# Two transformer blocks on one core: state-space branch with rows by token, its tables ordered behind half of the embeddings, and the input projection done by halves

## The chip, the cores and the metric

The kernel runs on one core of one Trainium2 chip, as one program. The metric is the device time of one execution in microseconds (us). The core's engines are TensorE (PE), VectorE (DVE), ScalarE (ACT), GpSimd (POOL) and SyncE (SP, which issues the DMAs). Each works through its own instructions in order and waits on semaphores for the others.

## The reference

Two blocks run one behind the other on x, 1024 tokens of 1024 channels, in fp32. The change lies in the first one.

```python
def first_block(x, ...):
    x = layer_norm(x, ln_emb_g, ln_emb_b)
    z = x @ w_in                                  # 1024 -> 1984 columns
    xs, gs, cq, ckv, kr, gm = split(z)            # 512, 512, 256, 128, 64, 512
    ys = s5_branch(xs, ...) * silu(gs)
    ym = mla_branch(cq, ckv, kr, cos, sin, ...) * silu(gm)
    u = alpha * x + concat(ys, ym) @ w_out
    return layer_norm(u + sigmoid(u @ w_pg) * (p @ w_pp), ln_g, ln_b)

def s5_branch(u, ...):        # 32 groups of 16 channels, 64 complex states for each group
    # a = exp(dt * A);  x_t = k * (B u_t);  h_t = a * h_(t-1) + x_t
    # y_t = Re(C h_t) + d * u_t;  y = gelu(y);  return y * sigmoid(y @ w_glu + b_glu)
```

The second block (adaptive normalisation, dilated attention, 2-D neighbourhood attention, a convolutional feed-forward network) is the longer part of the program.

## The kernel before

Matmul operands are split into a high and a low part (`split_sb`: a cast, and a subtraction for the rest), and each product is three matmuls (`mm3`, lines 135 to 137: high by high, high by low, low by high). `dense` walks over groups of column tiles `mt` of 128 columns, and for each over the two halves `th` of 512 tokens; a tile of `w_in` takes 8 steps of three matmuls, so 24.

The start of the program normalises x (`xt`, `mv`, `rs`), transposes it on PE (`tp`), scales it on ACT (`y`), casts it on DVE (`xh`) and takes the rest on POOL for odd channel tiles, on DVE for even ones (`xl`). PE also multiplies p by w_pp here (operands `ph` and `pl`, evacuated to `ppo`). DVE does at the same time, in `ssm_tables`, the tables of the state-space branch: `edt*` and `emg*` are exponentials, `ang`, `scs` and `scc` the sines and cosines, `pw` and `pv` the powers, `RA` and `RB` the two factors of the rotation of the scan.

The branch runs in eight units of four groups (`ssm_unit(u)`). Eight tokens times 16 channels are folded onto the 128 partitions, and 128 such steps are left. A unit loads `U`; builds `ES` and `CS` (a product on POOL, one on DVE into `tm`, and their sum on DVE); transposes `ES` on PE (`sps`, line 653, copied by ACT to `EM`); multiplies `CS` with `KR` on PE (`kps`, line 658). From `kps`, `TM` is built on DVE: it holds the influence of eight tokens on each other, so it is `kps` shifted by 0 to 7 places in eight bands of 16 rows, one masked instruction for each shift. Then PE gives `px` (line 690), DVE rotates it with `R` (`xr`), scans (`gg`, with the decay `RH`), rotates back (`h`), and PE adds `TM` by `U` and `CS` by `h` into `py` (lines 711 and 712). ACT applies gelu, and the result is stored.

The order of instructions on every engine is set at build time by a scheduler that walks the program with a timeline of its own. PE puts the remaining tiles of `w_in` (4 to 14), the rest of the attention's inputs and the units between each other. `after(a, b)` keeps b behind a in that order without a wait.

Of the kernel before, what the change touches and what calls it, by code (L numbers as in the profile page):

```python
# [37 lines left out]
CST = {}  # L38
_o = 0
for _n, _w in (("inv_freq", 1), ("sgn", 1), ("shift", 8), ("chan", 16)):  # L40
    CST[_n] = (_o, _w)
    _o += _w
# [5 lines left out]
def ap_of(t, offset, dims):  # L48
    return bass.AP(tensor=t.tensor, offset=t.offset + offset, ap=dims)


class Kernel:
# [112 lines left out]
    def dense(self, groups, src, nk, X, evac, psum, tag="mm", halves=(0, 1), pre=None, after=None, late=0,  # L165
              behind=None):


        n = 0
        for grp in groups:  # L170
            ws = pre or {mt: self.load_w(src(mt), nk * 128) for mt in grp}
            pre = None
            tiles = [(mt, th) for th in halves for mt in grp]

            cuts = [0, late, nk] if late else [0, nk]
            pss = {}
# [99 lines left out]
    def block1(self):  # L276
# [10 lines left out]
        xts, pre = [], {}  # L287
# [10 lines left out]
        for th in range(2):  # L298
# [325 lines left out]
    def ssm_unit(self, u):  # L624
# [1405 lines left out]
def _constants():  # L2030
# [47 lines left out]
def _layout(v):  # L2078
    A = np.ascontiguousarray
    f = {k: np.asarray(x) for k, x in v.items()}  # L2080
    r = {}
# [72 lines left out]
```

## Time and profile before

| what | value |
|---|---|
| median of 3 runs | 2269.06 us (2267.28 to 2270.81) |
| the profiled execution's own time | 2265.56 us |
| its span in the trace | 2263.5 us |
| mean granted TensorE clock | 0.972 |
| PE busy | 2122.7 us (94%) |
| DVE busy | 1502.9 us (66%) |
| POOL busy | 1124.1 us (50%) |
| ACT busy | 969.7 us (43%) |

The busy shares are means over stages with different limits. The branch that changes lies in the first 325 us, where PE has its longest pauses. The profiled execution was 3.5 us quicker than the median.

### The profile page before, as it was taken

The page shows a single profiled execution, that of the slowest core. Times are in us where ns is not written, and L with a number is a line of the kernel's source. Part 1 is how long each engine was busy: PE and PEld are TensorE (multiplying, and loading weights), DVE is VectorE, ACT ScalarE, POOL GpSimd, SP SyncE. Part 2 cuts the span into 40 slices and gives each one's busy share as a digit, 9 for nine tenths or more (in the row PEclk, how much of TensorE's full clock was granted, in tenths as well). Part 3 has the DMA queues.
Part 4 walks back from the last instruction along what each step waited for, and adds up shares of the span by engine and source line. Part 5 has one row for each costly group of instructions (what it writes and reads, how often), then busy time and mean ns, then how long its engine had stood idle before and what let it go on. Part 6 is the DMA issues. An engine that isn't in the chain of part 4 may idle for free.

```text
span 2263.5 us, 29117 instructions
## 1 busy us (share of the span) xinstructions
PE 2122.7 (94%) x10216; PEld 1766.0 (78%) x10216; DVE 1502.9 (66%) x2511; ACT 969.7 (43%) x1717; POOL 1124.1 (50%) x728
## 2 busy tenths in 40 slices
PE   5998999899999989999999898999899999989998
PEld 4776777777877778888887786888688888877887
DVE  8969976652486345545656862435987777777676
ACT  4222345432245356666444442223544444455223
POOL 4625556665554545654423333523455555535471
PEclk8999999999999999999999899999999999999999
DMA  7433345555654555555345545442122222234332
GB/s 274 137 101 108 92 122 177 177 172 182 199 172 166 175 167 170 171 171 150 121 136 158 166 159 181 169 139 102 47 84 84 84 84 84 84 130 135 98 126 80
DMA packets 186973, 313.25 MB, mean 138 GB/s; under 512 B 43512, under 2 KB 85068, under 8 KB 186828
## 3 DMA queue, kind: packets, MB, share of 16 engines
q1 hardware_dynamic: 186828, 311.40, 43.0%
q8 instruction: 80, 1.31, 0.2%
q14 instruction: 65, 0.53, 0.1%
HBM read 225.65 MB, written 80.96 MB: 135 GB/s over the span
## 4 chain that ended last, share of the span: by engine, by line
PE 41%; DVE 6%; DMA 2%; issue 1%; ACT 1%; POOL 1%; SPq 0%; POOLq 0%; DVEq 0%; ACTq 0%
PE u L1704 17%; PE ps L137 4%; PE ps L135 4%; PE ps L136 4%; PE pd L1885 3%; PE pd L136 2%; PE pd L135 2%; PE pd L137 2%; PE po L1386 1%; DMA ox<-o_d 1%; DVE P L90 1%; PE tp L1378 1%; DVE x L86 1%; DMA as<-a_d 1%; DVE a L86 1%
## 5 line engine op out<-in xcount | busy, mean ns | idle before, releaser
L111 POOL TENSOR_TENSOR wl<-wst,wh 128x1024 fp32r<-128x1024 f32 (+2 forms) x159 | 398.3, 2507 | 488.8 <-ACT wh L102 454.4
L102 ACT ACTIVATE wh<-wst 128x1024 fp32r<-128x1024 f32 (+1 forms) x164 | 168.3, 1028 | 274.2 <-PE ps L136 115.2
L83 POOL TENSOR_TENSOR acc<-acc,wa 128x512 f32<-128x512 f32 x84 | 110.5, 1316 | 16.6 <-ACT wa L102 13.3
L135 PE MATMUL ps<-xh,wh 128*128 128x512 f32 x256 | 103.3, 404 | 4.2 <-DVE kb L83 2.7
L135 PE MATMUL ps<-h1h,wh 128*128 128x512 f32 x256 | 102.5, 400 | 2.8 <-DVE qz L86 2.1
L135 PE MATMUL ps<-h0h,wh 128*128 128x512 f32 x256 | 103.9, 406 | 0.6 <-ACT wh L102 0.6
L137 PE MATMUL ps<-h0h,wl 128*128 128x512 f32 x256 | 102.9, 402 | 0.7 <-POOL wl L111 0.6
L136 PE MATMUL ps<-h0l,wh 128*128 128x512 f32 x256 | 103.1, 403 | 0.0
L136 PE MATMUL ps<-h1l,wh 128*128 128x512 f32 x256 | 102.7, 401 | 0.0
L137 PE MATMUL ps<-xh,wl 128*128 128x512 f32 x256 | 102.0, 399 | 0.0
L136 PE MATMUL ps<-xl,wh 128*128 128x512 f32 x256 | 101.9, 398 | 0.0
L137 PE MATMUL ps<-h1h,wl 128*128 128x512 f32 x256 | 101.9, 398 | 0.0
L83 POOL TENSOR_TENSOR tb<-rt,grid 128x384 f32<-128x384 f32 x48 | 43.1, 906 | 117.0 <-DVE mx L886 88.9
L135 PE MATMUL pd<-Ah,wh 128*128 128x512 f32 (+1 forms) x256 | 93.8, 366 | 5.4 <-ACT s L102 5.4
L136 PE MATMUL pd<-Al,wh 128*128 128x512 f32 (+1 forms) x256 | 93.8, 366 | 0.5 <-DVE Al L111 0.5
L137 PE MATMUL pd<-Ah,wl 128*128 128x512 f32 (+1 forms) x256 | 92.8, 366 | 0.0
L83 DVE TENSOR_TENSOR z<-r,wst 128x512 f32<-128x512 f32 x40 | 71.6, 1790 | 24.5 <-POOL wl L111 24.0
L886 DVE CUSTOM_DVE_ANT_0 sp<-sp,tab 128x256 f32<-128x256 f32 (+1 forms) x128 | 52.7, 425 | 41.8 <-PE sp L163 26.4
L90 POOL TENSOR_SCALAR wa<-wa,sc 128x512 f32<-128x512 f32 x36 | 56.9, 1582 | 47.0 <-DMA wa<-in_w_ada 45.3
L111 POOL TENSOR_TENSOR wl<-z,wh 128x1024 fp32r<-128x1024 f32 (+1 forms) x28 | 63.9, 2282 | 30.8 <-ACT wh L102 27.2
L102 ACT ACTIVATE a<-a 128x1024 f32<-128x1024 f32 x22 | 23.4, 1063 | 108.9 <-DVE a L86 108.8
L83 DVE TENSOR_TENSOR s<-s,pd 128x512 f32<-128x512 f32 x76 | 51.0, 681 | 27.9 <-PE pd L137 14.1
(595 smaller groups left out, 7086.3 us busy)
## 6 DMA issues: line engine op xcount, KB each, us to landing
wa<-in_w_ada SPq DMA_DIRECT2D x96, 256.0 KB, 3.1
wst<-in_w_in SPq DMA_DIRECT2D x47, 512.0 KB, 4.0
wst<-in_w_up SPq DMA_DIRECT2D x24, 512.0 KB, 3.3
a_d<-a SPq DMA_DIRECT2D x22, 512.0 KB, 2.6
wst<-in_w_down SPq DMA_DIRECT2D x22, 512.0 KB, 3.6
as<-a_d SPq DMA_DIRECT2D x22, 512.0 KB, 3.6
r<-in_w_up SPq DMA_DIRECT2D x20, 512.0 KB, 3.2
wst<-in_w_out SPq DMA_DIRECT2D x16, 512.0 KB, 3.3
```

The costliest lines, as they stand in the source:

```text
L83: (eng or self.nc.vector).tensor_tensor(out, a, b, op)
L86: self.nc.vector.scalar_tensor_tensor(out, a, s, b, op0=op0, op1=op1)
L90: (eng or self.nc.vector).tensor_scalar(out, a, s1, None, op0=op0)
L102: self.nc.scalar.activation(out, a, f, **kw)
L111: self.last_lo = e.tensor_tensor(lo, y, hi.bitcast(F32), ALU.subtract)
L135: first = mm(ps, wh, xh, start=start, stop=False)
L136: mm(ps, wh, xl, start=False, stop=False)
L137: mm(ps, wl, xh, start=False, stop=stop)
L886: self.nc.vector.tensor_tensor_reduce(out=s, in0=s, in1=tab, scale=-1.0, scalar=-NEG, op0=ALU.add, op1=ALU.min, accum_out=m)
L1378: nc.tensor.transpose(tp[:, g], P[:, g], self.ident)
L1704: nc.tensor.matmul(ps, x[:, s], y[:, k], start=first and n == 0, stop=k == 3 and n == 2, skip_group_check=True)
L1885: nc.tensor.matmul(ps, w[u][:, 128 * k:128 * k + 128], x[v], start=start and k == i == 0, stop=k == 1 and i == 2, skip_group_check=True)
```

## The change

1. Tiles 0 to 3 of `w_in` are one group, so their first half is done for all four before the second half of any.
2. The cast of odd channel tiles of the embeddings is done by ACT, 8 of 16.
3. The nine loads of the tables' inputs are ordered behind the store of the last tile of the first half of the embeddings.
4. `dd`, the skip term, is computed once for all 32 groups.
5. A row of the branch's tiles is token by channel instead of channel by token. `U` is loaded in four DMAs, `ES` and `KR` are laid out with channels innermost, so that `ES` is written without a stride.
6. `TM`: one masked product and one masked sum on DVE write `Z` (shift 0 or 1 by the row's parity), and four copies on ACT, of 32 rows each, put it at its place, shifted by 0, 2, 4, 6. The zeros are written once, by two memsets on POOL.
7. `RH`, a broadcast of the decay over 512 columns, goes from POOL to ACT; the memset of its first column stays.
8. `tm`, `x2`, `xr`, `gg`, `g2` and `h` have two buffers instead of one.

```diff
@@ dense
-            ws = pre or {mt: self.load_w(src(mt), nk * 128) for mt in grp}
+            ws = {mt: pre[mt] if pre and mt in pre else self.load_w(src(mt), nk * 128) for mt in grp}
@@ embeddings, loop over th (half) and ct (tile of 128 channels)
-                self.split_sb(y, XH[th][:, ct, :], XL[th][:, ct, :], "v", "g" if ct % 2 else "v")
-                nc.sync.dma_start(self.xn_d[ct][:, th * 512:(th + 1) * 512], y)
+                self.split_sb(y, XH[th][:, ct, :], XL[th][:, ct, :], "a" if ct % 2 else "v", "g" if ct % 2 else "v")
+                st = nc.sync.dma_start(self.xn_d[ct][:, th * 512:(th + 1) * 512], y)
+            if th == 0:
+                half = st
-        self.ssm_tables()
+        self.ssm_tables(half)
@@ projection
-        self.dense([[0, 1], [2, 3]], src, 8, X, evac, pp, pre=pre)
+        self.dense([[0, 1, 2, 3]], src, 8, X, evac, pp, pre=pre)
@@ ssm_open
+        self.TM = [self.sp2.tile([128, 4, 16, 8], F32, name=f"TM{i}") for i in range(2)]
+        for x in self.TM:
+            self.nc.gpsimd.memset(x, 0.0)
@@ ssm_tables(behind): each of the nine loads alike
-        nc.sync.dma_start(prm, I["ssm_prm"])
+        self.after(behind, nc.sync.dma_start(prm, I["ssm_prm"]))
...
+        self.dd = K("dd", [128, 32, 16])
+        self.tt(self.dd, dsk[:, :, None].to_broadcast([128, 32, 16]),
+                self.cst[:, None, o:o + 16].to_broadcast([128, 32, 16]), ALU.mult)
@@ ssm_unit
-        nc.sync.dma_start(U, ap_of(self.u_d[b], 64 * q * 1024, [[128, 128], [16 * 1024, 4], [1, 128]]))
-
-        ES = T("ES", [128, 4, 16, 8])
+        for g in range(4):
+            nc.sync.dma_start(U[:, g], ap_of(self.u_d[b], (64 * q + 16 * g) * 1024, [[128, 8], [1024, 16], [1, 128]]))
+
+        ES = T("ES", [128, 4, 8, 16])
...
-            o, t = (y.rearrange("p g c e -> p g e c") for y in (out, tm))
+            tm = T("tm", list(out.shape), 2)
+            o, t = (y if out is ES else y.rearrange("p g c e -> p g e c") for y in (out, tm))
...
-        dd = T("dd", [128, 4, 16])
-        self.tt(dd, self.dsk[:, G][:, :, None].to_broadcast([128, 4, 16]),
-                self.cst[:, None, o:o + 16].to_broadcast([128, 4, 16]), ALU.mult)
-        self.tt(ps[:, :, :, 0], ps[:, :, :, 0], dd, ALU.add)
-        TM = T("TM", [128, 4, 16, 8], 2)
-        o = CST["shift"][0]
-        self.ts(TM, ps, self.cst[:, o:o + 1], None, ALU.mult)
-        for s in range(1, 8):
-            self.stt(TM[:, :, :, s:], ps[:, :, :, :8 - s], self.cst[:, o + s:o + s + 1], TM[:, :, :, s:], ALU.mult,
-                     ALU.add)
+        self.tt(ps[:, :, :, 0], ps[:, :, :, 0], self.dd[:, G], ALU.add)
+
+        Z = T("Z", [128, 4, 16, 8])
+        m = [self.cst[:, CST[n][0]:CST[n][0] + 1] for n in ("even", "odd")]
+        self.ts(Z, ps, m[0], None, ALU.mult)
+        self.stt(Z[:, :, :, 1:], ps[:, :, :, :7], m[1], Z[:, :, :, 1:], ALU.mult, ALU.add)
+        TM = self.TM[u % 2]
+        for k in range(4):
+            r = slice(32 * k, 32 * k + 32)
+            self.act(TM[r, :, :, 2 * k:], Z[r, :, :, :8 - 2 * k], AF.Copy)
...
-        self.ts(RH, self.rho[:, G][:, :, None].to_broadcast([128, 4, 128]), 1.0, None, ALU.mult, eng=nc.gpsimd)
+        self.act(RH, self.rho[:, G][:, :, None].to_broadcast([128, 4, 128]), AF.Copy)
...
-        x2 = T("x2", [128, 4, 128])
+        x2 = T("x2", [128, 4, 128], 2)
```

The constants follow the new row order. Three places show what the scheduler makes of this.

DVE, in the middle of the embeddings, where the first instruction of the tables (`edtr`, from the load `prm`) stands; before:

```order
L303 BN_STATS st<-xt 128x6 x2
L92 TENSOR_SCALAR xt<-xt,mv,rs 128x1024 x2
L92 TENSOR_SCALAR edtr<-prm 128x32
L83 TENSOR_TENSOR den<-prm 128x32
L83 TENSOR_TENSOR t_796<-prm 128x32
L305 BN_AGGR mv<-st 128x2 x2
L92 TENSOR_SCALAR edta<-edtr 128x32
L83 TENSOR_TENSOR den<-den,t_796 128x32
```

and in the change (`xh_124`/`xl_126` are the first half's, `xh_125`/`xl_127` the second half's operands):

```order
L111 TENSOR_TENSOR xl_126<-y,xh_124 128x512
L92 TENSOR_SCALAR xt<-xt,mv,rs 128x1024 x2
L107 CAST xh_124<-y 128x512
L111 TENSOR_TENSOR xl_126<-y,xh_124 128x512
L107 CAST xh_125<-y 128x512
L111 TENSOR_TENSOR xl_127<-y,xh_125 128x512
L92 TENSOR_SCALAR edtr<-prm 128x32
L83 TENSOR_TENSOR den<-prm 128x32
L83 TENSOR_TENSOR t_798<-prm 128x32
L92 TENSOR_SCALAR edta<-edtr 128x32
```

The tables' first instruction has moved from behind the fourth pair of normalised rows to behind the casts of the whole first half and one of the second.

PE, at the end of tiles 0 to 3 of `w_in`, where unit 0 begins; `lps` is a small product for the second block; before:

```order
L137 MATMUL ps<-xh_125,wl 128x512
L955 MATMUL lps<-oh,rel 8x383
L653 MATMUL sps<-ident,ES 128x128 x4
L658 MATMUL kps<-CS,KR 128x128 x4
L955 MATMUL lps<-oh,rel 8x511
L135 MATMUL ps<-xh_124,wh 128x512
...
L136 MATMUL ps<-xl_126,wh 128x512
L690 MATMUL px<-U,EM 128x128 x4
L137 MATMUL ps<-xh_124,wl 128x512
```

and in the change:

```order
L137 MATMUL ps<-xh_125,wl 128x512
L967 MATMUL lps<-oh,rel 8x383
L666 MATMUL sps<-ident,ES 128x128 x4
L671 MATMUL kps<-CS,KR 128x128 x4
L702 MATMUL px<-U,EM 128x128 x4
L967 MATMUL lps<-oh,rel 8x511
L135 MATMUL ps<-xh_124,wh 128x512
```

Unit 0's `px` has moved from 17 matmuls into tile 4 to directly behind `kps`.

DVE, unit 1, from `kps` on (`z` belongs to the attention's inputs); before:

```order
L83 TENSOR_TENSOR kps<-kps,dd 128x64
L90 TENSOR_SCALAR TM<-kps,cst 128x512
L83 TENSOR_TENSOR dd<-dsk,cst 128x64
L83 TENSOR_TENSOR ES<-ES,tm 128x512
L86 SCALAR_TENSOR_TENSOR TM<-kps,cst,TM 128x64x7
L83 TENSOR_TENSOR tm<-C_607,pw 128x4x8x16
L86 SCALAR_TENSOR_TENSOR TM<-kps,cst,TM 128x64x6
L83 TENSOR_TENSOR CS<-CS,tm 128x512
L86 SCALAR_TENSOR_TENSOR TM<-kps,cst,TM 128x64x5
L86 SCALAR_TENSOR_TENSOR z<-z,vecs,rb 128x512
L83 TENSOR_TENSOR tm<-kB_815,pv 128x4x8x16
L86 SCALAR_TENSOR_TENSOR TM<-kps,cst,TM 128x64x4
```

and in the change:

```order
L83 TENSOR_TENSOR kps<-kps,dd 128x64
L90 TENSOR_SCALAR Z<-kps,cst 128x512
L83 TENSOR_TENSOR ES<-ES,tm 128x512
L86 SCALAR_TENSOR_TENSOR Z<-kps,cst,Z 128x64x7
L83 TENSOR_TENSOR tm<-C_607,pw 128x4x8x16
L86 SCALAR_TENSOR_TENSOR z<-z,vecs,rb 128x512
L83 TENSOR_TENSOR xr<-px,R 128x512
L83 TENSOR_TENSOR x_1490<-x_1490,R 128x512
```

The masked sums of `TM` are gone but for one. On ACT there stands in their place, in the change:

```order
L102 ACTIVATE EM<-sps 128x512
L102 ACTIVATE KR<-kB_816 128x512
L102 ACTIVATE TM_1106<-Z 32x512
L102 ACTIVATE TM_1106<-Z 32x64x6
L102 ACTIVATE TM_1106<-Z 32x64x4
L102 ACTIVATE TM_1106<-Z 32x64x2
L102 ACTIVATE ckh<-z 128x512
L102 ACTIVATE x_1490<-px 64x512 x2
```

The four copies stand ahead of `ckh` and of unit 1's two copies of `px`.

## Rows read from the trace of the kernel before

**Rows 1.** Busy time by stretch; columns: stretch, us, engines with counts, TensorE clock, DMA share, GB/s.

```profile
20.40:67.10 46.70, 32.66 (x127) 24.87 (x126) 46.60 (x108) 21.65 (x33) 28.83 (x16) 0.79 0.67 230
67.10:112.00 44.90, 44.90 (x200) 36.48 (x199) 44.45 (x108) 10.35 (x15) 29.47 (x16) 1.00 0.47 127
112.00:160.30 48.30, 45.23 (x233) 37.60 (x231) 28.21 (x41) 14.06 (x26) 14.55 (x12) 0.96 0.42 120
160.30:231.20 70.90, 59.61 (x289) 48.97 (x288) 70.22 (x98) 22.54 (x35) 35.41 (x24) 0.93 0.32 95
231.20:325.00 93.80, 85.86 (x440) 71.65 (x440) 78.55 (x111) 30.13 (x49) 41.74 (x27) 0.98 0.35 99
325.00:2263.50 1938.50, 1845.45 (x8901) 1539.28 (x8901) 1220.99 (x2013) 864.25 (x1556) 970.65 (x628) 0.98 0.43 138
```

**Rows 2.** Timeline of DVE; columns: start us, us busy, engine, line, operation.

```profile
20.46 0.18 DVE L92 TENSOR_SCALAR edtr<-prm 128x32 f32<-128x32 f32 x1
...
108.51 2.56 DVE L83 TENSOR_TENSOR CS<-CS,tm 128x512 f32<-128x512 f32 x1
```

**Rows 3.** Timeline of PE around state-space unit 0; columns as in the group above.

```profile
111.98 1.06 PE L658 MATMUL kps<-CS,KR 128*128 128x128 f32 x8
114.05 1.01 PE L955 MATMUL lps<-oh,rel 34*8 34x511 f32 x2 [1.01 <-DMA oh<-in_oh]
114.99 0.50 PE L135 MATMUL ps<-xh,wh 128*128 128x512 f32 x1
...
118.98 1.05 PE L690 MATMUL px<-U,EM 128*128 128x128 f32 x8
```

**Rows 4.** Chain of waits of PE, 160.3 to 231.2: line, for whom: us, times, longest.

```profile
PE px L690 <- DVE xr L83: 3.7, 1, 3.7
PE ps L135 <- DVE kb L83: 2.7, 2, 2.0
PE ps L135 <- DVE qa L83: 2.7, 2, 1.5
```

**Rows 5.** The same of PE from 231.2 to 325.

```profile
PE py L712 <- DVE h L83: 6.0, 4, 1.9
```

**Rows 6.** Tile views: count, duration ns min/median/max, first and last start us, shape.

```profile
L86 DVE SCALAR_TENSOR_TENSOR TM<-kps,cst,TM x56: 309/476/684, 121.6 to 308.2; 128x448 f32<-128x448 f32 x8, 128x384 f32<-128x384 f32 x8, 128x320 f32<-128x320 f32 x8, 128x256 f32<-128x256 f32 x8
L90 DVE TENSOR_SCALAR TM<-kps,cst x8: 720/738/752, 120.8 to 300.6; 128x512 f32<-128x512 f32 x8
...
L83 DVE TENSOR_TENSOR h<-gg,g x8: 672/1137/2874, 134.2 to 309.8; 128x508 f32<-128x508 f32 x8
...
L90 POOL TENSOR_SCALAR RH<-rho x8: 1494/1582/1780, 101.7 to 292.2; 128x512 f32<-128x512 f32 x8
```

**Rows 7.** DVE instructions by shape, 0 to 325: count, busy us, mean ns, idle before.

```profile
L83 DVE TENSOR_TENSOR rt<-RA,RB 128x512 f32<-128x512 f32 x16 | 17.2, 1077 | 0.2
L83 DVE TENSOR_TENSOR tm<-kB,pv 128x512 f32<-128x512 f32 x8 | 10.4, 1296 | 0.0
L107 DVE CAST xh<-y 128x512 fp32r<-128x512 f32 x16 | 8.7, 554 | 0.0
L86 DVE SCALAR_TENSOR_TENSOR TM<-kps,cst,TM 128x448 f32<-128x448 f32 x8 | 5.4, 671 | 0.0
L83 DVE TENSOR_TENSOR dd<-dsk,cst 128x64 f32<-128x64 f32 x8 | 2.3, 291 | 0.0
```

**Rows 8.** ACT instructions by shape, the same stretch and columns.

```profile
L102 ACT ACTIVATE x<-px 64x512 f32<-64x512 f32 x16 | 9.5, 594 | 28.0 <-DVE h L83 12.5 <-PE px L690 10.5 <-issue 4.9
```

**Rows 9.** Tile view of the load of U, on SP's queue.

```profile
L633 SPq DMA_DIRECT2D U<-u_d x8: 371/386/913, 89.6 to 285.2; - x8
```

**Rows 10.** Timeline of PE after a pause in the first stage.

```profile
43.59 0.80 PE L136 MATMUL ps<-pl,wh 128*128 128x512 f32 x1 [3.13 <-POOL pl L111]
45.89 0.63 PE L136 MATMUL ps<-pl,wh 128*128 128x512 f32 x1
...
47.33 0.39 PE L136 MATMUL ps<-pl,wh 128*128 128x512 f32 x1
```

More of the change, by code (lines that the diff above doesn't have):

```diff
@@ L39 @@
 _o = 0
-for _n, _w in (("inv_freq", 1), ("sgn", 1), ("shift", 8), ("chan", 16)):
+for _n, _w in (("inv_freq", 1), ("sgn", 1), ("even", 1), ("odd", 1), ("chan", 16)):
     CST[_n] = (_o, _w)
@@ L507, in sincos, with ssm_tables @@
         return k, z
-    def ssm_tables(self):
+    def ssm_tables(self, behind):
         nc, I, keep = self.nc, self.I, self.sp
@@ L514, in ssm_tables @@
         prm = T("prm", [128, 3, 32])
-        nc.sync.dma_start(prm, I["ssm_prm"])
+        self.after(behind, nc.sync.dma_start(prm, I["ssm_prm"]))
         bc = T("bc", [128, 2, 32, 16])
-        nc.sync.dma_start(bc, I["ssm_bc"][:, :2])
+        self.after(behind, nc.sync.dma_start(bc, I["ssm_bc"][:, :2]))
         self.Cs = K("Cs", [128, 32, 16])
-        nc.sync.dma_start(self.Cs, I["ssm_bc"][:, 2])
+        self.after(behind, nc.sync.dma_start(self.Cs, I["ssm_bc"][:, 2]))
         self.C2 = K("C2", [128, 32, 16])
-        nc.sync.dma_start(self.C2, I["ssm_bc"][:, 3])
-        self.dsk = K("dsk", [128, 32])
-        nc.sync.dma_start(self.dsk, I["ssm_d"])
+        self.after(behind, nc.sync.dma_start(self.C2, I["ssm_bc"][:, 3]))
+        dsk = T("dsk", [128, 32])
+        self.after(behind, nc.sync.dma_start(dsk, I["ssm_d"]))
+        o = CST["chan"][0]
+        self.dd = K("dd", [128, 32, 16])
+        self.tt(self.dd, dsk[:, :, None].to_broadcast([128, 32, 16]),
+                self.cst[:, None, o:o + 16].to_broadcast([128, 32, 16]), ALU.mult)
         pos = T("pos", [128, 256], I32)
         for q in range(4):
-            nc.sync.dma_start(pos[32 * q:32 * q + 32, :],
-                              ap_of(I["pos"], 256 * q, [[0, 32], [1, 256]]))
+            self.after(behind, nc.sync.dma_start(pos[32 * q:32 * q + 32, :],
+                                                 ap_of(I["pos"], 256 * q, [[0, 32], [1, 256]])))
         sgn = self.cst[:, CST["sgn"][0]:CST["sgn"][0] + 1]
@@ L632, in ssm_unit @@
         U = T("U", [128, 4, 128], 2)
-        nc.sync.dma_start(U, ap_of(self.u_d[b], 64 * q * 1024, [[128, 128], [16 * 1024, 4], [1, 128]]))
-        ES = T("ES", [128, 4, 16, 8])
+        for g in range(4):
+            nc.sync.dma_start(U[:, g], ap_of(self.u_d[b], (64 * q + 16 * g) * 1024, [[128, 8], [1024, 16], [1, 128]]))
+        ES = T("ES", [128, 4, 8, 16])
         CS = T("CS", [128, 4, 16, 8], 2)
-        tm = T("tm", [128, 4, 16, 8])
         for out, pw, a, c, op in ((ES, self.pv, self.kB1, self.kB2, ALU.add),
                                   (CS, self.pw, self.Cs, self.C2, ALU.subtract)):
-            o, t = (y.rearrange("p g c e -> p g e c") for y in (out, tm))
+            tm = T("tm", list(out.shape), 2)
+            o, t = (y if out is ES else y.rearrange("p g c e -> p g e c") for y in (out, tm))
             sh = [128, 4, 8, 16]
@@ L647, in ssm_unit @@
             self.tt(out, out, tm, op)
-        KR = T("KR", [128, 4, 16, 8])
-        self.act(KR, self.kB1[:, G][:, :, :, None].to_broadcast([128, 4, 16, 8]), AF.Copy)
+        KR = T("KR", [128, 4, 8, 16])
+        self.act(KR, self.kB1[:, G][:, :, None, :].to_broadcast([128, 4, 8, 16]), AF.Copy)
         EM = T("EM", [128, 4, 128], 2)
@@ L690, in ssm_unit @@
             nc.tensor.matmul(px[:, g, :], EM[:, g, :], U[:, g, :], start=True, stop=True)
-        x2 = T("x2", [128, 4, 128])
+        x2 = T("x2", [128, 4, 128], 2)
         self.act(x2[0:64], px[64:128], AF.Copy)
         self.act(x2[64:128], px[0:64], AF.Copy)
-        xr = T("xr", [128, 4, 128])
+        xr = T("xr", [128, 4, 128], 2)
         self.tt(xr, px, rc, ALU.mult)
@@ L698, in ssm_unit @@
         self.tt(xr, xr, x2, ALU.subtract)
-        gg = T("gg", [128, 4, 128])
+        gg = T("gg", [128, 4, 128], 2)
         nc.vector.tensor_tensor_scan(f(gg), f(RH), f(xr), 0.0, op0=ALU.mult, op1=ALU.add)
-        g2 = T("g2", [128, 4, 128], 1, "x2")
+        g2 = T("g2", [128, 4, 128], 2, "x2")
         self.act(g2[0:64], gg[64:128], AF.Copy)
         self.act(g2[64:128], gg[0:64], AF.Copy)
-        h = T("h", [128, 4, 128])
+        h = T("h", [128, 4, 128], 2)
         nc.vector.memset(h[:, :, 0:1], 0.0)
@@ L2049, in _constants @@
     cst[:, CST["sgn"][0]] = np.where(k < 64, -1.0, 1.0)
-    o, w = CST["shift"]
-    cst[:, o:o + w] = k[:, None] % 8 == np.arange(8)[None]
+    cst[:, CST["even"][0]] = k // 16 % 2 == 0
+    cst[:, CST["odd"][0]] = k // 16 % 2 == 1
     o, w = CST["chan"]
-    cst[:, o:o + w] = k[:, None] // 8 == np.arange(16)[None]
+    cst[:, o:o + w] = k[:, None] % 16 == np.arange(16)[None]
     oh = np.zeros((34, L1W + L2W), np.float32)
@@ L2096, in _layout @@
     r["ssm_bc"] = A(np.stack([np.concatenate(t) for t in ((br, bi), (bi, br), (cr, ci), (ci, cr))], 1))
-    r["ssm_d"] = A(np.repeat(f["d_skip"][0].reshape(32, 16).T, 8, axis=0))
+    r["ssm_d"] = A(np.tile(f["d_skip"][0].reshape(32, 16).T, (8, 1)))
     r["w_glu"] = A(_tiles(f["w_glu"][0]))
```

1 line of the change is left out of this document (removed).

## The prediction

> **What bounds the kernel now.** I read the busy times by stretch first. Over the whole span PE is the engine with the least to spare, so a gain must come out of PE's pauses, and the stretches say where these are [rows 1]. From 325 us on PE is busy 1845.45 of 1938.5 us, and nothing of the change works there. Before that it has pauses in four places: 14.0 us between 20.4 and 67.1, 3.1 between 112 and 160.3, 11.3 between 160.3 and 231.2, and 7.9 between 231.2 and 325. Between 67.1 and 112 it has none: these are tiles 0 to 3 of `w_in`.
>
> Next, who is late. DVE is busy 46.60 of 46.70 us in the first of these stretches, 44.45 of 44.90 in the second and 70.22 of 70.90 in the fourth [rows 1]; ACT works less than half of each, 22.54 of 70.90 in the fourth. The waits agree: between 160.3 and 231.2 PE waits for `xr`, `kb` and `qa`, all of DVE [rows 4], and after 231.2 mostly for `h`, 6.0 us [rows 5]. The timeline of DVE shows the head: the tables begin at 20.46, and the last thing that unit 0's `kps` needs, `CS`, ends at 108.51 + 2.56 = 111.07 [rows 2]; `kps` starts at 111.98 [rows 3], when PE has just finished the four tiles. So in the kernel before, DVE's chain and PE's chain meet at about 111 us, by chance of balance, and from there on DVE is behind. Pulling PE alone forward in the head gives nothing: it would wait for `CS`.
>
> **The head, to the start of tile 4.** The order says what DVE does before unit 0's first `CS`. Since it has no pause there, the end of `CS` moves by the work that is taken out and put in, wherever the pieces stand. Eight of 16 casts go: 8 x 0.554 = -4.4 us [rows 7]. The whole `dd` (512 wide, at the 0.671 of the 448-wide sum, its nearest row) replaces one of 0.291: +0.4. One more `tm` (unit 1's) stands ahead of `CS`: +1.1, the mean of the contiguous `rt`. The two `tm` of `ES` lose their stride: 2 x (1.296 - 1.077) = -0.4. That is -3.3. POOL's first `RH` ran from 101.7 [rows 6], beside the instructions that make `CS`, and that `CS` took 2.56 where `rt`'s mean is 1.08; without `RH` I take 1.0 off. Against it stand new waits: the embeddings are now packed, so DVE may wait for ACT's `y` and for `prm`: +1.0, a choice, since DVE shows no such wait to read from; bounds 0 and 5. `CS` then ends at about 107.8.
>
> PE starts tiles 0 to 3 earlier, because the embeddings no longer share DVE with the tables: somewhere between 46 and 57 by my reading, 67.1 before. The tiles take 44 us, so PE is at unit 0 between 91 and 102 and waits for `CS`. From `CS` on it is `kps` 1.06, `px` 1.05 (now here) and the second `lps`, 0.94 to the start of tile 4 [rows 3]: 110.9. Before, tile 4 started at 114.99 and still had `px` ahead: 116.0. So -5.1. The pause costs clock: after the 3.13 us pause at 43.59 seven matmuls ran at 0.63 us and not at 0.39 [rows 10], the lower level of 1.2 GHz, so +1.6. **Head: -3.5**, bounds -12 (PE meets no pause) and +3 (the gain is eaten by DVE waits of 5 and by a longer spell of low clock).
>
> **112 to 160.** `px` stands 17 matmuls earlier, so unit 0 asks for its operands sooner; `TM` goes over ACT. The four copies are not in the trace: the nearest row is the 64-row, 512-wide copy of `px`, 0.594 [rows 8]. Four at that price are 2.4 us, by width about 1.8 (1 + 3/4 + 1/2 + 1/4 of it is 1.5, with a fixed part more); nothing to 2.4 are the bounds. DVE's part of `TM` falls from 0.738 and seven sums of median 0.476, so 4.1 us [rows 6], to 0.738 + 0.671 = 1.4 [rows 7]. The path from `kps` to `TM` is then 1.4 + 1.8 and no longer interleaved with other work, so shorter than before. I take **+1** for the earlier demand, bounds -2 and +2.
>
> **160 to 231, three units.** Per unit DVE loses 4.1 - 1.4 = 2.7 for `TM`, 0.3 for `dd`, 0.2 for `ES`'s `tm`, but consecutive DVE rows overlap by a little under 0.1 us and six instructions go, so I take 2.8. Three units: 8.4. POOL's `RH`, 1.58 each [rows 6], goes to ACT, where a 512-wide copy lies in ACT's 48 us of idle time. What DVE gets back from that I put at half: 2.4 of 4.7. DVE then needs 70.2 - 10.8 = 59.4, PE's own busy time is 59.61: they meet, and neither can be filled quite. Of PE's 11.3 us of pauses I take **-8.5**, bounds -3 (the next DVE result in line becomes late instead) and -11.
>
> First the row on that half: the `TM` instructions, with one operand in PSUM, went from 0.309 to 0.684 by width and were never longer, while `h`, with two in SBUF, went from 0.672 to 2.874 in one shape [rows 6]. The Trainium skill, SBUF — State Buffer, section Who interferes with whom, states that a DVE instruction with two SBUF inputs contends with a GpSimd instruction that reads SBUF, and one with at most one such input does not; the rows agree. By that rule alone, everything that `RH` occupies could come back, and this stage's term would be -11 rather than -8.5, the whole 2250.5; it also says that the removed `TM` sums free their bare time only.
>
> **231 to 325, four units.** DVE has 78.55 of 93.80 busy, so the shed work counts only where PE waits: 7.9 us, 6.0 of them for `h`. `h` is late by a chain (`px`, two copies, rotation, scan, two copies, rotation) of which the change takes nothing but queueing; second buffers let the next unit's front run earlier. **-4.5**, bounds -1 and -6.5.
>
> **Costed at nothing.** Three more issues for each `U`, 0.386 on SP each [rows 9], 24 in all, 9.3 us spread over 200: the loads stand a unit ahead. If this cover were gone, one unit would wait 1.2. Two memsets of `TM` on POOL stand ahead of unit 0's `ES`, when PE is at tiles 0 to 3. Tiles 2 and 3 of `w_in` have their loads and splits earlier. The four copies stand ahead of two copies of `px` on ACT; if `Z` were late, `px`'s copies and then `xr` would be late by the same. After 325 the order moves in small pieces only: 0, bounds -3 and +3.
>
> **Sum.** -3.5 + 1 - 8.5 - 4.5 = -15.5. The profiled execution's own time is 2265.56, 3.5 below the median; so 2250.1 by it, and by the median 2269.06 - 15.5, so about **2253.5**. Differences under 0.2%, 4.5 us, can't be told from no change here.
>
> **Rivals.**
> (1) DVE's chain to `CS` shrinks far more. Many of its rows in the head are long by collision, as `CS` with 2.56; with the tables moved to where POOL only splits weights and multiplies, they could be shorter. If `CS` ended at 97, PE would hardly pause: head -14 in place of -3.5, with no clock lost; since PE then asks sooner for the rest, about 2 is lost again: 2245. Against it: POOL's work in these stretches, 28.8 and 29.5 us [rows 1], is nearly the same.
> (2) The shed work is swallowed. DVE's order is fixed, PE's too; if what PE waits for after `TM` (`xr`, `kb`, `qa`, `h`) stays late for reasons of chain and not of load, the terms of the two later stages shrink to -3 and -1: -6.5, 2262.5. For it: none of the longest waits of PE there is for `TM` [rows 4, 5]. That the order of the loads doesn't decide where the tables stand is no case: the order shows them moved.
> (3) Slower. The tables start where the embeddings end; their first instruction moves from 20.46 to about 38, my estimate from the embeddings' instructions that now stand ahead of it. If DVE's room in the packed embeddings is lost in waits for PE and ACT, so that the whole 17.5 us carries through, `CS` ends at 128.6 and the head is 128.6 + 3.1 + 1.6 - 116.0 = +17.3. With +1 - 8.5 - 4.5 that is +5.3: 2274.4. It decides against the change from `CS` at about 123 on. For it: the chain from `edtr` to `CS` has long stretches of small dependent instructions. Against: DVE's 91 us there were full, and the embeddings' part doesn't vanish, it moves ahead.
>
> **How the numbers follow.** My forecast 0.60, (1) 0.12, (2) 0.16, (3) 0.12. The forecast's own range, by the terms' bounds taken half, is 2245 to 2261. The range that leaves out two in ten reaches to most of (1) and (2) and leaves out (3) and the far ends: 2241 to 2266. Faster by over 0.2%: the forecast but for 0.03, (1), and two thirds of (2): 0.79. Same: 0.03 + 0.05 + 0.03 of (3): 0.11. Slower: 0.10, the rest of (3) and mishaps at far bounds.
>
> **What would show it.** `edtr` near 38 and unit 0's `CS` ending near 108; tiles 0 to 3 starting around 50 and PE pausing 6 to 16 us for `sps` or `kps`, then some matmuls at the low clock; tile 4 at about 111. DVE less than 62 us busy in what was 160 to 231, with PE's waits for `xr`, `kb` and `qa` under 4 together. Copies of `TM` on ACT of 0.3 to 0.6. I am wrong if `CS` is later than 115, if PE's waits in the units have only changed their names, or if the part after unit 7 is longer or shorter by more than 3.

## The result and the profile after

The changed kernel takes 2286.36 us (median of 4 runs, 2284.01 to 2289.12), the kernel before 2268.17 (4 runs): ratio 1.0083 [1.0071, 1.0096], so 18 to 19 us slower. The forecast was 2253.5 and the range 2241 to 2266. The profiled execution took 2288.44, its span is 2286.5, the clock 0.971.

The busy times by stretch, as in [rows 1]; the stretches begin behind the first transposes of the embeddings, at the second matmul of `w_in` and the second of its tile 4, and at the matmuls that stood at 160.2, 232.8 and 325.5 before:

```profile
21.80:52.90 31.10, 25.75 (x123) 20.52 (x122) 29.00 (x45) 22.96 (x37) 25.53 (x16) 0.91 0.82 272
52.90:116.40 63.50, 52.66 (x217) 40.60 (x216) 62.84 (x162) 16.01 (x25) 30.49 (x18) 0.89 0.41 123
116.40:160.10 43.70, 42.84 (x212) 35.26 (x211) 23.39 (x35) 12.94 (x25) 9.83 (x10) 0.96 0.44 124
160.10:223.50 63.40, 59.15 (x289) 48.69 (x288) 59.15 (x72) 27.22 (x45) 29.22 (x22) 0.95 0.31 96
223.50:323.35 99.85, 88.26 (x447) 72.42 (x446) 69.07 (x86) 42.31 (x74) 38.94 (x28) 0.97 0.34 101
323.35:2286.50 1963.15, 1863.24 (x8899) 1543.23 (x8897) 1224.69 (x2012) 864.96 (x1555) 965.67 (x623) 0.98 0.42 137
```

At 323.35 us the changed kernel is 2.2 us ahead of 325.53 before. The loss lies behind that point, where no instruction of the change works: PE is busy 17.8 us longer (1863.24 against 1845.45) for the same number of matmuls (8899 against 8901), and pauses some 7 us longer (99.9 against 93.1), which the account below takes up under 325 to 545. The next fences narrow the longer busy time to one stage of the second block's feed-forward network, where PE never pauses and the clock is full. Windows (columns as in [rows 1]) of before:

```profile
1900.00:2000.00 100.00, 100.00 (x443) 82.84 (x442) 76.72 (x68) 44.48 (x53) 53.59 (x25) 1.00 0.23 80
```

and of after, the same stretch of matmuls, moved by one or two of them:

```profile
1914.60:2017.00 102.40, 102.40 (x443) 82.94 (x442) 76.63 (x69) 44.38 (x52) 53.61 (x25) 1.00 0.22 78
```

2.4 us more for 443 matmuls are 5.4 ns each in the mean. PE's timeline (start, duration) shows them one by one; before:

```profile
1800.57 0.39 PE L1704 MATMUL u<-b11h,wl 128*128 128x512 f32 x1
1800.80 0.39 PE L1704 MATMUL u<-t2h,wh 128*128 128x512 f32 x1
1801.03 0.39 PE L1704 MATMUL u<-t2l,wh 128*128 128x512 f32 x1
1801.25 0.39 PE L1704 MATMUL u<-t1h,wh 128*128 128x512 f32 x1
1801.48 0.39 PE L1704 MATMUL u<-t1l,wh 128*128 128x512 f32 x1
1801.70 0.39 PE L1704 MATMUL u<-t4h,wh 128*128 128x512 f32 x1
```

and after:

```profile
1813.22 0.39 PE L1716 MATMUL u<-b11h,wl 128*128 128x512 f32 x1
1813.44 0.40 PE L1716 MATMUL u<-t2h,wh 128*128 128x512 f32 x1
1813.68 0.40 PE L1716 MATMUL u<-t2l,wh 128*128 128x512 f32 x1
1813.91 0.40 PE L1716 MATMUL u<-t1h,wh 128*128 128x512 f32 x1
1814.14 0.40 PE L1716 MATMUL u<-t1l,wh 128*128 128x512 f32 x1
1814.38 0.40 PE L1716 MATMUL u<-t4h,wh 128*128 128x512 f32 x1
```

From `t2h` to `t4h` are four steps: 0.90 us before, 0.94 after. The `b11h` matmul ahead of them takes its old 0.22 to 0.23. So it goes by the operand, and not by the stage.

What these operands share is their place in SBUF. The change cuts the constants' tile `cst` from 26 to 20 columns, a part of the diff that stands ahead of this section only as "the constants follow":

```diff
-for _n, _w in (("inv_freq", 1), ("sgn", 1), ("shift", 8), ("chan", 16)):
+for _n, _w in (("inv_freq", 1), ("sgn", 1), ("even", 1), ("odd", 1), ("chan", 16)):
```

104 bytes become 80; in the built programs the tile occupies 128 and then 96 bytes, and all that is allocated behind it on that side moves down by 32 bytes (`xh` from byte 3808 of each partition to 3776). The weights `wh` and `wl` lie on the other side and stay. I sorted the 7356 matmuls of 512 columns by the address of the moving operand less that of the weights, modulo 256, and took the mean distance from one start to the next, where no pause lies between, from the trace:

| kernel | difference 0 | other differences |
|---|---|---|
| before | 6588 matmuls, 227.8 ns | 384 at 32 and 384 at 192, both 233.3 |
| after | 3324, 228.2 ns | 3648 at 224, 233.3; 384 at 192, 233.3 |

`xh` went from 227.8 to 233.2, `mh` from 226.8 to 233.3, `t1h` from 226.8 to 233.4; `h0h`, which did not move against its weights, from 229.6 to 228.9; and `uh`, 32 off before, came into place: 233.4 to 227.0. `b11h`, in place in both, went from 226.8 to 228.3; nothing here explains that smaller step.

The stretch of the change, by PE's waits up to 400 us (line, for whom: us, times, longest):

```profile
PE ps L135 <- ACT wh L102: 10.5, 3, 9.0
PE sps L666 <- DVE ES L83: 8.9, 1, 8.9
PE py L723 <- ACT TM L102: 8.0, 2, 7.2
...
PE ps L135 <- DVE qa L83: 2.3, 1, 2.3
...
PE kps L671 <- DVE CS L83: 1.9, 1, 1.9
...
PE px L702 <- DMA U<-u_d: 0.8, 2, 0.5
...
PE py L724 <- DVE h L83: 0.5, 1, 0.5
```

and for `TM` in the same view of before:

```profile
PE py L711 <- DVE TM L86: 4.3, 3, 2.1
```

`xr` and `kb` of [rows 4] are gone and `qa` is left. Of the 6.0 us for `h` of [rows 5] 0.5 are left; the waits for `TM` have grown from 4.3 us to 8.0, and one of them is 7.2 long. The four loads for each `U`, costed at nothing, cost PE 0.8.

### The profile page after: what moved, and what is told of

The parts are those of the page before. It is cut to its first block, busy times and chain, and to the rows that moved or that the text cites. A ratio compares the mean times of both kernels' runs of the same rounds, so it can differ in the third digit from the quotient of the medians.

```text
span 2286.5 us, 29126 instructions
## 1 busy us (share of the span) xinstructions
PE 2142.3 (94%) x10216; PEld 1768.9 (77%) x10216; DVE 1483.0 (65%) x2448; ACT 993.7 (43%) x1765; POOL 1103.5 (48%) x722
## 4 chain that ended last, share of the span: by engine, by line
PE 43%; DVE 6%; DMA 1%; ACT 1%; issue 1%; SPq 0%; POOL 0%; POOLq 0%; DVEq 0%; ACTq 0%
PE u L1716 17%; PE ps L137 5%; PE ps L135 5%; PE ps L136 5%; PE pd L1897 3%; PE pd L136 2%; PE pd L135 2%; PE pd L137 2%; PE po L1398 1%; PE tp L1390 1%; DVE x L86 1%; DVE P L90 1%; DVE a L86 1%; PE sp L162 0%; DVE kl L83 0%
## 5 line engine op out<-in xcount | busy, mean ns | idle before, releaser
L898 DVE CUSTOM_DVE_ANT_0 sp<-sp,tab 128x256 f32<-128x256 f32 (+1 forms) x128 | 52.6, 425 | 37.2 <-PE sp L163 21.7
```

What stands on the lines that cost most here:

```text
L898: self.nc.vector.tensor_tensor_reduce(out=s, in0=s, in1=tab, scale=-1.0, scalar=-NEG, op0=ALU.add, op1=ALU.min, accum_out=m)
```

## The experiments

Ratios are to the kernel before, run beside it on the same chip, with 95% intervals. `a_fz` and `a_fz2` below differ by 0.2% for the same work, so a difference of that size between two experiments says little.

**Is it the place of the operands?** Three kernels. In the first (`a_pad`), the change with the constants' tile at its old size:

```diff
+for _n, _w in (("inv_freq", 1), ("sgn", 1), ("even", 1), ("odd", 1), ("chan", 16), ("pad", 6)):
```

> The changed kernel, with six unused columns put back at the end of the constants' tile (26 columns as before, not 20), so that every tile behind it lies 32 bytes higher again; no instruction moves. Theory 1 (phase): a 512-wide matmul follows the last one after 227 ns when its moving operand and its weights lie at the same place modulo 128 bytes, and after 233 ns when not; the change put 4032 of 7356 such matmuls out of phase, 768 were before. 3264 matmuls at 5.2 to 6.3 ns are 17 to 20.6 us: about 2266 to 2269 here, near the kernel before. Rival (the lost time lies in the change's own work: the copies of TM on ACT, waits, queues): within 3 us of the changed kernel, 2286.

Measured: 2274.91 us, 1.0018 [1.0008, 1.0029]. In the second (`b_shift`), the kernel before with eight columns more, so that all lies 32 bytes higher:

```diff
+for _n, _w in (("inv_freq", 1), ("sgn", 1), ("shift", 8), ("chan", 16), ("pad", 8)):
```

> The kernel before, with eight unused columns added to the constants' tile, so that the tiles behind it lie 32 bytes higher; nothing else differs. Theory 1: 4416 of 7356 matmuls out of phase in place of 768, 3648 at 5.2 to 6.3 ns: 19 to 23 us longer, about 2287 to 2291, without any part of the change. Rival: no difference from the kernel before.

Measured: 2286.85 us, 1.0069 [1.0056, 1.0082]; the stage that took 530.0 us before (from the matmul at 1480.1 to that at 2010.1) takes 541.4, and 540.4 in the changed kernel. In the third (`a_wshift`), the change as it is, with the weights moved by the same 32 bytes and the constants left small:

```diff
+        self.open("pad", "right").tile([128, 8], F32, name="pad")
         self.wp = self.open("w", "right")
```

> The changed kernel with a tile of 32 bytes ahead of the pool of the weights, so that weights and all pools on that side lie 32 bytes lower, and in phase with the embeddings again; the constants stay at 20 columns. Theory 1 in its form that the relation of the two operands decides: as with the constants padded, 2266 to 2269. Its other form, that the moving operand must lie at 96 modulo 128 by itself: all 7356 are slow, about 21 us over the changed kernel, 2307. Rival (own work of the change): 2286.

Measured: 2275.21 us, 1.0019 [1.0008, 1.0029]. In the built programs of `a_pad` and `a_wshift` the counts are those of before, 6588 at difference 0; in `b_shift` 3648 lie at 32, 384 at 64 and 384 at 192. The three agree: the loss comes without the change and goes with the change kept, and the difference between operand and weights decides, not where either lies. From 1.0018 to 1.0083 are 0.0065 of 2270, **14.8 us**, by the two intervals some 11 to 18. By count, 4032 less 768 matmuls at 5.4 ns would be 17.6. `b_shift` loses 15.7, where 19 to 23 were expected, and the interval of `a_pad` lies above 1: the places are most of the loss, but not all of it.

**How far can it be had?** The kernel before and `a_pad` both have tiles out of place (`uh`, `ul`, and `cq`, `ckh`, `ys1`, `ymh`). A pad in front of each of two pools moves them, on top of the old size of `cst`. First I took 128 bytes for the period (`a_best`):

```diff
+        self.cqp.tile([128, 16], F32, name="cqpad")
...
+        up.tile([128, 24], F32, name="upad")
```

> The changed kernel with the constants padded as in the first, and 64 and 96 unused bytes in the pools of cq and of uh, so that all 7356 matmuls are in phase. Theory 1: 768 matmuls at 6.3 ns less than with the constants alone, so 4 to 5 us: about 2261 to 2264. Rival: no difference from the first.

Measured: 2278.94 us, 1.0033 [1.002, 1.0045]. A miss: `uh` stood 128 bytes off and kept 233.2 ns, `cq` 231.9. With 256 (`cqpad` of 48 columns, `upad` of 56), for the change (`a_best2`) and for the kernel before (`b_best2`):

> The changed kernel with the constants padded, and 192 and 224 unused bytes in the pools of cq and of uh. The run with 64 and 96 bytes left uh and cq at 233 and 232 ns though they lay at the same place modulo 128 as the weights; at 256 they did not. Theory 1 in its second form (the same place modulo 256): all 7356 matmuls are in phase, uh at 227 ns, and 768 x 6.3 ns = 4.8 us come off the constants alone: about 2270 where that gave 2274.9. Rival (uh and cq are slow for another reason, such as what runs beside them): uh stays at 233 ns, no gain.

> The kernel before with the same two pads, nothing of the change: by theory 1 all 7356 in phase and 4.8 us off: 2267 where the kernel before has 2271.9. Rival: no difference.

Measured: the change 2275.02 us, 1.001 [0.9998, 1.0022]; the kernel before 2270.32, 0.9987 [0.9973, 1.0001]. All 7356 matmuls are now at difference 0 (`uh` 227.0, `ymh` 226.9). By count 768 x 5.4 = 4.1 us were to be had, the medians give some 2 and 3, which their intervals hardly separate from nothing. With the places equal, the change itself is 0.1 to 0.3% slower than the kernel before, and not 15.5 us faster.

**The tables' order by itself** (`a_free`). `ssm_tables(None)`, with the old size of `cst`: the loads are free again, all else is kept.

> The changed kernel with the constants padded, and the nine loads of the tables no longer ordered behind the first half: the tables' first instruction stands at place 37 of DVE's order as before, not 63. Theory 2: with the loads held back PE reaches unit 0 ten us too early, pauses, and then runs for 17 us at half clock, which costs about 4.5 us. Here PE should reach tiles 0 to 3 later, pause under 3 us for ES and CS, and show no long spell of half clock at 100 to 118: tile 4 of w_in about 3 to 5 us sooner, about 2270 to 2272. Rival: the pause is only moved into the head, the start of tile 4 is the same, 2275.

Measured: 2274.74 us, 1.0012 [0.9996, 1.0028]. `w_in` starts where it did before, and a new wait stands behind unit 0:

```profile
112.41 1.06 PE L673 MATMUL kps<-CS,KR 128*128 128x128 f32 x8
117.88 1.24 PE L969 MATMUL lps<-oh,rel 34*8 34x511 f32 x2 [4.42 <-DMA oh<-in_oh]
```

Both parts of the expectation fail: tile 4 starts at 119.05, 3.8 us later than in `a_pad` and not 3 to 5 sooner, and the half clock is not gone but stands from 119 to 122 (0.51). So putting the tables behind the first half neither costs nor gains that can be measured.

**`TM` on DVE again** (`a_dvetm`). The kernel after, with eight masked instructions as before (the mask now by `k // 16`, its columns restoring the size of `cst`), all else kept:

```diff
-        self.ts(Z, ps, m[0], None, ALU.mult)
...
+        self.ts(TM, ps, self.cst[:, o:o + 1], None, ALU.mult)
+        for s in range(1, 8):
+            self.stt(TM[:, :, :, s:], ps[:, :, :, :8 - s], self.cst[:, o + s:o + s + 1], TM[:, :, :, s:], ALU.mult,
+                     ALU.add)
```

> The changed kernel with the constants' tile at its old size and TM built by eight masked instructions on DVE as before, on the new rows. Theory 3: the 7.3 us that PE waits for TM in unit 3 come from the order that the scheduler makes when TM is cheap (kps waits 12 us in DVE's line behind R and CS, while py stands 35 matmuls earlier on PE): here that wait falls under 2 us, but DVE has 2.5 us more for each unit, so the end of unit 7 is within 3 us of the padded change and the time 2272 to 2278. Rival: the shed DVE work was worth its price, and the time is 2280 or more; or the copies on ACT cost all of it, and it is 2268 or less.

Measured: 2276.99 us, 1.0021 [1.0007, 1.0034]. The units from 160 to 325 of before take 160.5 us, 162.6 with `TM` over ACT (kernel `a_pad`). PE waits for `TM` here too, in shorter pieces (chain of waits, up to 400 us):

```profile
PE py L718 <- DVE TM L86: 11.9, 4, 5.1
```

The expected wait of under 2 us did not come, so the way over ACT is not what makes `TM` late. And with 1.0021 here and 1.0018 in `a_pad`, moving `TM` from DVE to ACT has no effect on the time that can be measured.

**Filling PE's pause, and `Z` first.** Tile 4 of `w_in` is done ahead of unit 0 (`a_fill`); or `R` and the next unit's `tm` are kept behind `Z` in DVE's order (`a_zf`); or both (`a_fz`). All three have the places of `a_best2`. In `a_fill` and `a_fz` the sums of squares for the norm of `cq` pair the wrong halves of its two tiles, with the same number of instructions.

```diff
-        self.dense([[0, 1, 2, 3]], src, 8, X, evac, pp, pre=pre)
+        self.dense([[0, 1, 2, 3], [4]], src, 8, X, evac, pp, pre=pre)
...
-        self.dense([[4, 5], [6]], src, 8, X, evac, pp)
+        self.dense([[5], [6]], src, 8, X, evac, pp)
```

```diff
-            self.tt(t, x(c), w(1), ALU.mult)
+            m = nc.vector.tensor_tensor(t, x(c), w(1), ALU.mult)
+            if self.lz:
+                self.after(self.lz, m)
...
-        self.tt(v(t1), A(1), B(1), ALU.mult)
+        m = nc.vector.tensor_tensor(v(t1), A(1), B(1), ALU.mult)
+        self.after(z, m)
```

(`z` is the unit's own masked sum into `Z`, `self.lz` that of the unit before.)

> The changed kernel, all matmuls in phase, with tile 4 of w_in put ahead of unit 0 in the program: 48 matmuls, 10.9 us, stand on PE between tile 3 and unit 0's transposes, where PE paused for about 11.5 us. Theory 2 (a pause there costs a spell of half clock of 14 to 17 us and so 4 to 5 us, beside the pause itself): no half clock at 100 to 118, PE comes to tile 5 some 10 us sooner; a part of it comes back as waits of units 1 to 3 for DVE, so 4 to 10 us off 2275: 2265 to 2271. Rival (DVE sets the pace from here on): the waits only move behind unit 0, 2273 to 2277.

> The changed kernel, all matmuls in phase, with DVE's order held so that a unit's kps and Z come ahead of its own R and of the next unit's tables (order only, no wait added). Theory 3 (the 7.3 us that PE waits for TM of unit 3 come from Z's place in DVE's line): no wait for TM over 2 us, 231 to 325 shorter by 4 to 7 us, 2268 to 2271. Rival: the waits go to px, h or ES of the next unit, which are now late, 2273 or more.

> Both of the last two. If theories 2 and 3 hold and add up: 2258 to 2266, ahead of the kernel before with all matmuls in phase (2270). If DVE sets the pace: no better than the better of the two alone.

Measured: 2269.62 us, 0.9987 [0.9971, 1.0004]; 2269.96, 0.9994 [0.9981, 1.0007]; 2264.46, 0.997 [0.9957, 0.9984]. Each is worth 3 to 5 us against `a_best2`, together about 9; only the two together are well clear of the intervals. `a_fill` has the expected time, but not by the expected path: the half clock moved behind unit 0 instead of going (0.52 from 112 to 118.5, 0.50 from there to 125), behind a new pause of 3.90 for `zq`, and tile 5 starts at 130.1, later than the 122.2 of `a_best2`. That it is 5.3 us ahead at the matmul of 325.5 is measured; what gives it these is open. In `a_zf` the stretch from 160 to 325 takes 158.8 us for 162.6; no wait for `TM` is left among those of 0.7 and more, and `h` is late instead, as its rival said, but by less than was won (chain of waits of PE, 157 to 317):

```profile
PE py L729 <- DVE h L83: 11.8, 5, 5.8
PE kps L675 <- DVE CS L83: 1.2, 1, 1.2
```

Both edits again, with the halves paired as in the reference (`a_fz2`: `zs[h::2]` in place of `zs[2 * h:2 * h + 2]`):

> The version with tile 4 ahead of unit 0 and Z ahead of the next tables, all matmuls in phase, with the sums of squares of cq taken from the halves in their new order, so that it computes the reference. The work is the same as in the run of both edits: 2262 to 2267, and faster than the kernel before by 0.2 to 0.4%. If theories 2 and 3 were an accident of that run: 2270 or more.

Measured: 2261.59 us, **0.995 [0.9938, 0.9962]**, faster than both kernels, and than the kernel before with its operands in place (0.9987 [0.9973, 1.0001]). PE's timeline shows that unit 0 no longer stalls for `ES` and `CS`; the pauses behind it are for `zq` and `oh` now:

```profile
107.77 0.60 PE L670 MATMUL sps<-ident,ES 128*128 128x128 f32 x4
108.20 1.06 PE L675 MATMUL kps<-CS,KR 128*128 128x128 f32 x8
110.84 0.38 PE L199 MATMUL rs<-ones_d,zq 128*128 128x1 f32 x2 [1.58 <-ACT zq L102]
117.22 1.43 PE L972 MATMUL lps<-oh,rel 34*8 34x383 f32 x2 [5.99 <-DMA oh<-in_oh]
```

## Why the prediction was wrong, point by point

Start of the same matmul in each trace, named by its time before; in the last rows the distance between two such points. A stage of one execution varies by a few us, as the pauses and the clock fall; and the execution of before that was profiled, 2265.56, lies 6.7 under the median that `a_best2` is compared with, so that the end of `a_best2` looks 9.9 us later where the medians differ by 2.7.

| point or stretch | before | after | `a_pad` | `a_best2` | `a_fz2` |
|---|---|---|---|---|---|
| first `w_in` matmul | 67.1 | 52.7 | 52.7 | 52.5 | 52.6 |
| tile 4 (in `a_fz2` ahead of unit 0) | 115.0 | 115.8 | 115.2 | 115.2 | 96.1 |
| 160.2 | 160.2 | 160.1 | 159.0 | 159.0 | 155.4 |
| 232.8 | 232.8 | 223.5 | 221.9 | 221.9 | 228.5 |
| 325.5 | 325.5 | 323.4 | 321.6 | 321.6 | 314.9 |
| 325.5 to 545.2 | 219.7 | 226.5 | 230.8 | 229.9 | 232.3 |
| 545.2 to 1480.1 | 934.9 | 937.2 | 939.3 | 937.3 | 931.7 |
| 1480.1 to 2010.1 | 530.0 | 540.4 | 530.8 | 530.4 | 530.2 |
| 2010.1 to 2256.2 | 246.0 | 251.7 | 247.3 | 246.9 | 243.0 |

**"After 325 the order moves in small pieces only: 0, bounds -3 and +3": this step failed**, and with it the sign, for up to 325.5 every form of the change is ahead of before. It looked at the order and not at the addresses; and with the addresses restored the stretch from 325 to 545 alone is still longer by more than its bound of 3. The prediction had named this as a sign of being wrong: a part after unit 7 longer by more than 3. The size of one small tile cost 14.8 us; in the profiled execution the last two stretches, where next to all operands had moved, are 10.4 and 5.7 above before. Three kernels show it: the size undone, the shift given to the kernel before, the weights moved after.

**The four terms up to 325, -15.5 forecast, -3.9 measured.** With the places restored (`a_pad`) they are -0.8 for the head, -0.4, -9.6 and +6.9. So the forecast would have failed without the addresses as well: the head's gain did not come, and the last term had the wrong sign.

**The head, -3.5 forecast, about 0 measured** (tile 4 at 115.83, against 116.0 with `px`). `w_in` started at 52.7 ("between 46 and 57"). `edtr` came at 44.81 and not near 38; of that, 1.25 us were a wait:

```profile
44.81 0.18 DVE L92 TENSOR_SCALAR edtr<-prm 128x32 f32<-128x32 f32 x1 [1.25 <-DMA prm<-in_ssm_prm]
```

DVE's waits in the head were this one and 0.61 for `y`, 1.9 where 1.0 was put; `CS` itself took 1.53, the 1.0 less that was taken off for `RH`. `CS` nonetheless ended at 108.66 + 1.53 = 110.19 instead of 107.8; which of the other instructions were longer than priced was not taken apart. Rival (3), the whole delay carried through to 128.6, did not occur. PE paused 8.94 + 1.90 us, within the 6 to 16 expected, and then ran slowly (timeline of PE, as [rows 3]):

```profile
107.33 1.11 PE L666 MATMUL sps<-ident,ES 128*128 128x128 f32 x4 [8.94 <-DVE ES L83]
110.34 2.05 PE L671 MATMUL kps<-CS,KR 128*128 128x128 f32 x8 [1.90 <-DVE CS L83]
112.18 1.92 PE L702 MATMUL px<-U,EM 128*128 128x128 f32 x8
114.03 1.87 PE L967 MATMUL lps<-oh,rel 34*8 34x511 f32 x2
115.83 0.80 PE L135 MATMUL ps<-xh,wh 128*128 128x512 f32 x1
116.42 0.63 PE L136 MATMUL ps<-xl,wh 128*128 128x512 f32 x1
```

From `kps` to tile 4 are 5.49 us, priced at 1.06 + 1.05 + 0.94 = 3.05 from rows at the full clock. I had put the clock's price at seven matmuls of tile 4, 1.6 (in [rows 10] five of the seven took 0.63, the first 0.80 and the last 0.49); the unit's own instructions, 2.4 more, ran at half clock as well. With `CS` 2.4 later, the head's gain is gone.

**112 to 160, +1 forecast.** Tile 4 to the matmul of 160.2 takes 43.8 us in `a_pad`, 45.3 before, of which `px`, now ahead, is 1.05. So -0.4: small, as said.

**160 to 231, -8.5 forecast, -9.6 measured** (63.0 us in `a_pad`, 72.5 before). DVE is busy 59.15 of 63.40 us in the changed kernel, 59.4 were forecast; PE's waits for `xr`, `kb` and `qa` are 2.3, under 4 as said; the copies on ACT take 0.31 to 0.63 (tile view; min, median, max in ns):

```profile
L102 ACT ACTIVATE TM<-Z x32: 314/476/634, 123.4 to 299.8; 32x512 f32<-32x512 f32 x8, 32x384 f32<-32x384 f32 x8, 32x256 f32<-32x256 f32 x8, 32x128 f32<-32x128 f32 x8
```

But of the 9.6 only 6.6 are pauses of PE (4.7 left of 11.3); 3 us of matmuls have moved on into the next stretch, so the term is right in sum and too large in kind. Nor is it the shed `TM` alone: with `TM` back on DVE (`a_dvetm`) the stretch takes 66.4 us, so 6.2 of the 9.6 come without it. That the term came out so near is in part luck. The other price that the prediction gives for this stage, -11 and the whole 2250.5, is added up wrongly (with -11 it is 2251.0), and did not come either.

**231 to 325, -4.5 forecast, +6.9 measured** (99.7 us in `a_pad`, 92.7 before). This term had the wrong sign. 3 us of the 6.9 are those matmuls; the rest are pauses, 12.6 us in `a_pad` for 8.5, and the largest is a wait of over 7 for `TM` (7.23 in the changed kernel), where none before was over 2.1. DVE's timeline in the changed kernel, in unit 3:

```profile
224.68 1.79 DVE L83 TENSOR_TENSOR R<-R,rt 128x512 f32<-128x512 f32 x1
226.39 2.88 DVE L83 TENSOR_TENSOR CS<-CS,tm 128x512 f32<-128x512 f32 x1
229.19 0.68 DVE L83 TENSOR_TENSOR rt<-RA,RB 128x512 f32<-128x512 f32 x1
229.79 1.07 DVE L83 TENSOR_TENSOR tm<-C,pw 128x512 f32<-128x512 f32 x1
230.69 0.28 DVE L83 TENSOR_TENSOR kps<-kps,dd 128x64 f32<-128x64 f32 x1
231.01 0.75 DVE L90 TENSOR_SCALAR Z<-kps,cst 128x512 f32<-128x512 f32 x1
```

and PE's:

```profile
217.90 0.83 PE L671 MATMUL kps<-CS,KR 128*128 128x128 f32 x6
...
235.34 0.79 PE L723 MATMUL py<-U,TM 128*128 128x128 f32 x2 [7.23 <-ACT TM L102]
```

PE went on to its next product at 218.49, with `kps` behind it. DVE came to it at 230.69, because `R` and the `CS` of the next unit stood ahead in its order; `Z` and the copies follow, and PE waits 7.23 us. I had expected the second buffers to let the next unit's front run earlier; it ran ahead of this unit's end. That the buffers are what allowed it wasn't tried. That the order makes this wait `a_zf` shows, which turns it: the wait is gone, and both stretches together take 158.8 us for 162.6 in `a_best2`. With it gone the two are 6.5 us shorter than the 165.3 of before, still not the 13 that were forecast; `h` is what PE waits for then.

The long `CS` also bears on the half of `RH` that I left open. `R` took 0.66 us where POOL was idle (at 214.93 in `a_pad`), but 1.79 and `CS` 2.88 here, beside this (timeline of POOL):

```profile
223.09 5.63 POOL L111 TENSOR_TENSOR wl<-wst,wh 128x1024 fp32r<-128x1024 f32 x2
```

`RH` has left POOL, but POOL still works beside these instructions, here on a split of weights. What the move of `RH` gave by itself was not tried. The rule of the Trainium skill (SBUF — State Buffer, Who interferes with whom), that a DVE instruction with two SBUF inputs contends with a GpSimd instruction that reads SBUF, agrees with these rows.

**325 to 545, costed at nothing, +7 to +13.** The changed kernel and the ten made from it take 226.5 to 232.3 us here, the kernel before 219.7, `b_best2` 220.2 and `b_shift` 224.0; so some 4 us can come without the change. In `a_best2` it is pauses: PE is busy 199.74 us before and 200.60 there. In `a_pad` half of it is a busy time of 205.7, at a granted clock of 0.95 where before has 0.98. The attention's code there is unchanged, but the scheduler has arranged it anew: about a tenth of the 1115 matmuls stand elsewhere in PE's order, where `b_best2` and `b_shift` have the order of before. PE waits longer for some things (`ptl` 5.4 us in `a_best2` for 2.3, `P` 3.8 for 1.7, `wh` 4.0 for 2.3). No experiment isolated one, so which move does it stays open.

Of the rivals, (3) has the nearest number once the places are restored, 2274.4, and `a_best2` has 2275.02; that is luck, since its `CS` at 128.6 did not come. In mechanism (2), the shed work swallowed, is nearest, with 2262.5. Its reason was half right: a result in DVE's line was late, but through order, not through a chain.

## What to carry to other kernels

A change that resizes a tile at the bottom of an allocator's side moves every tile behind it. Before costing instructions, compare the addresses of the matmuls' operands in both built programs; pad the tile back, or the comparison measures the move and not the change. Where a scheduler may run the next unit earlier, look in its order at what now stands before a result that another engine already waits for. Price a pause of PE with all that runs at half clock behind it.

## What the runs showed of the hardware

A 512-column fp32r matmul is followed by the next after 227 ns (median; mean 227.8 in the kernel before) if its moving operand and its weights lie at the same place modulo 256 bytes (3648 of the 6588 there lie an odd multiple of 256 apart, and step no slower than the others), and after 233.3 ns at differences of 32, 192 or 224 (3648 matmuls at 224 alone); `uh` at 128 kept 233.2. At 64 (in `b_shift`) it took 229.0, for 227.0 in place; but some operands in place take as long (`h0h` 229.6), so that says little. The Trainium skill, SBUF — State Buffer, Who interferes with whom, gives PE one read port for the moving operand and another, independent one for weight loads; by that the relation of their places would not matter. It matters here, and the measurement decides. Which access meets which was not tried.

In `a_pad` PE pauses 9.61 and 1.90 us at unit 0 (8.94 and 1.90 in the changed kernel). The granted clock was 0.53 from 112.0 to 118.5, about the lower level of 1.2 GHz, and full at 2.4 GHz in the stretch behind it:

```profile
98.00:112.00 14.00, 3.39 (x15) 3.02 (x15) 13.86 (x13) 5.09 (x9) 13.16 (x10) 0.61 0.35 91
112.00:118.50 6.50, 6.50 (x18) 3.92 (x18) 6.40 (x6) 2.27 (x4) 4.34 (x2) 0.53 0.08 23
118.50:159.00 40.50, 39.02 (x206) 32.87 (x204) 20.87 (x32) 12.85 (x24) 8.77 (x9) 1.00 0.51 133
```
